# Row scaling in pieces and TensorE transposes ahead of the first projection, with dummy products while x is loaded

## The chip, the cores and the metric

The kernel runs on one core of a Trainium2 chip. The metric is the device time of one execution in microseconds (us); lower is better. The engines are named as the profile names them: PE (TensorE products) and PEld (its weight loads), DVE (VectorE), ACT (ScalarE), POOL (GpSimd), and the queues that issue DMAs (SPq, ACTq, POOLq).

## The reference

One decoder layer on 512 tokens of width 1024, in f32. The part that the change touches is the very beginning:

```
h    = x * rsqrt(mean(x*x, axis=-1) + 1e-6) * attn_norm
proj = h @ w_in     # columns: attention q, k, v | RWKV r, k, v, loras | memory q
```

Behind it come differential attention, an RWKV-7 time mix (a chunked delta-rule recurrence), cross-attention into a normalised memory, one output projection with a residual, and a mixture of 16 experts with top-2 routing. These are the same in both kernels.

## The kernel before, in words

**Arithmetic.** Every large product is computed from pairs: an operand is split into a rounded high part and the rest, and three products (high-high, high-low, low-high) are added in PSUM (`mm3`, L242 to L245; in the first unit written out at L341 to L343). A weight chunk of 128 x 1024 is loaded by SPq into `raw`, ACT copies it into `whi` (L96), DVE subtracts to give `wlo` (L97).

**Beginning.** x is four tiles of 128 tokens by 1024 columns, `xt[0]` to `xt[3]`. Tiles 0 and 1 form half 0, tiles 2 and 3 half 1. For each tile `row_root` (L275) sums the squares (DVE at L279 for one tile of a half, ACT at L281 for the other) and POOL makes the root with a power of -0.5 (L282, L283). PE must turn x so that its columns lie on partitions. The kernel before does this by a product: `half_turn` (L324) multiplies each 128 x 128 block of x with `diag[t]`, a diagonal matrix of the tile's row factors, so that scaling and turning are one f32 product. `diag` is made from the identity by DVE for half 0 (L348) and by ACT for half 1 (L364). One `half_turn(n)` covers 128 columns of the two tiles of a half; n from 0 to 7 is half 0, 8 to 15 is half 1. `half_split` (L330) multiplies the turned block with the norm's gain and splits it into `h_hi` (ACT, L291) and `h_lo` (DVE, L292). `half_products` (L335) then multiplies column block k of a half with the first 256 columns of w_in: six products of 256 columns per k, 48 per half.

**Order.** The block from L345 to L374 stands in a manual schedule: ACT, DVE and PE carry out what is written there in that order. POOL and SPq are not under it. In the kernel before PE's order is: turns 0 to 7, products of half 0 for k 0 to 3, turns 8 to 11, products of half 0 for k 4 to 7, turns 12 to 15, products of half 1. All work behind it (`projections`, `rwkv`, `attention`, the experts) is ordered by a planner that simulates the engines' times, from generators that are woven by estimated delays (`Weave`); the next unit's products (L243 to L245) follow on PE, and a root pair for the memory tile goes through DVE, POOL and ACT (L279, L282, L283, L287). POOL's long list of small preparations (`later()`, L380) may start only when the last root of x is there.

**Banks.** The turned blocks go through six PSUM banks, used by halves: two of `pt`, two of `pc`, two of `pp` (L319). The bank of block n is used again 12 blocks later.

Of the kernel before, what the change touches and what calls it, by code (L numbers as in the profile page):

```python
# [12 lines left out]
BF = mybir.dt.bfloat16  # L13
I32 = mybir.dt.int32
AF = mybir.ActivationFunctionType
ALU = mybir.AluOpType
# [4 lines left out]
P = 128  # L21
S = 512
D = 1024
NT = S // P
KC = D // P
# [125 lines left out]
def hybrid_layer_kernel(ctx, tc, x, mem, positions, cols, w_in, w_kv, w_out, wa2, g2, ffn, wr, br,  # L151
                        wg, wu, wd, out):
    nc = tc.nc
    V, A, G, T = nc.vector, nc.scalar, nc.gpsimd, nc.tensor
# [3 lines left out]
    rc = ctx.enter_context(tc.tile_pool(name="rc", bufs=1))  # L158
# [12 lines left out]
    def pp():  # L171
        return psp.tile([P, 512], F32, name="pp", bufs=4)

    def pc():
        return pools["ps"].tile([P, 512], F32, name="pc", bufs=2)
# [18 lines left out]
    def b4(name, shape, dtype=F32):  # L194
        return biga.tile(shape, dtype, name=name)
# [4 lines left out]
    xt = [xs[t // 2][:, t % 2, :] for t in range(NT)]  # L200
# [4 lines left out]
    ident = const.tile([P, P], F32, name="ident")  # L205
# [69 lines left out]
    def row_root(src, vec=True):  # L275
        ss = wk.tile([P, 1], F32, name="ssx", bufs=4)
        r = wk.tile([P, 1], F32, name="rsx", bufs=4)
        if vec:
            V.tensor_tensor_reduce(b4("aw0", [P, D]), src, src, 1.0, 0.0, op0=ALU.mult, op1=ALU.add, accum_out=ss)  # L279
        else:  # L280
            A.activation(b4("aw1", [P, D]), src, AF.Square, accum_out=ss)  # L281
        G.tensor_scalar(r, ss, 1.0 / D, RMS_EPS, op0=ALU.mult, op1=ALU.add)  # L282
        return r, G.tensor_tensor(r, r, mhalf, op=ALU.pow)  # L283
# [6 lines left out]
    def split_cols(ps, g, hi, lo):  # L290
        first = A.activation(hi, ps, AF.Copy, scale=g)  # L291
        return first, V.scalar_tensor_tensor(lo, ps, g, hi.bitcast(F32), op0=ALU.mult, op1=ALU.subtract)  # L292


    held = [ws.pair.pop() for _ in range(4)]
    ws.pump()
    for t in (2, 3):
        nc.sync.dma_start(xt[t], x[t * P:(t + 1) * P, :])
# [5 lines left out]
    dint = post_[:, S:2 * S]  # L304
    nc.sync.dma_start(posr, bass.AP(tensor=positions.tensor, offset=positions.offset, ap=[[0, P], [1, S]]))
    nc.sync.dma_start(posc, positions.rearrange("o (t p) -> p (o t)", p=P))
    diags = [b4(f"qmT{t}", [P, 2, P]) for t in range(2)]
    diag = [diags[t // 2][:, t % 2, :] for t in range(NT)]
    first_ps = [pp() for _ in range(2)]
    first_w = []  # L310

    def weights():
        ws.pair.append(held.pop())
        ws.pump()
        first_w.append(ws.use())
# [3 lines left out]
    def half_bank(n):  # L319
        if n % 12 < 6 and len(banks) <= n // 12 * 6 + n % 6:  # L320
            banks.append((pt, pt, pc, pc, pp, pp)[n % 6]())
        return banks[n // 12 * 6 + n % 6][:, n % 12 // 6 * 256:n % 12 // 6 * 256 + 256]

    def half_turn(n):  # L324
        hf, k = divmod(n, KC)
        o = half_bank(n)
        for t in range(2):
            T.matmul(o[:, t * P:(t + 1) * P], xt[2 * hf + t][:, k * P:(k + 1) * P], diag[2 * hf + t], start=True, stop=True)

    def half_split(n):  # L330
        hf, k = divmod(n, KC)
        tk = slice(hf * 256, hf * 256 + 256)
        return split_cols(half_bank(n), col[:, C_AN + k:C_AN + k + 1], h_hi[:, k, tk], h_lo[:, k, tk])

    def half_products(hf, ks):  # L335
        tk = slice(hf * 256, hf * 256 + 256)
        for k in ks:
            hi, lo = first_w[k // 4]
            for j in range(2):
                o, wh, wl = first_ps[j][:, tk], hi[:, k % 4, j * P:(j + 1) * P], lo[:, k % 4, j * P:(j + 1) * P]  # L340
                T.matmul(o, wh, h_hi[:, k, tk], start=hf == 0 and k == 0, stop=False, skip_group_check=True)  # L341
                T.matmul(o, wh, h_lo[:, k, tk], start=False, stop=False, skip_group_check=True)
                T.matmul(o, wl, h_hi[:, k, tk], start=False, stop=k == KC - 1, skip_group_check=True)  # L343

    with tc.manual_schedule(engines={mybir.EngineType.Activation, mybir.EngineType.DVE, mybir.EngineType.PE}):  # L345
        roots = [row_root(xt[0]), row_root(xt[1], False)]
        for t in range(2):
            V.tensor_scalar(diag[t], ident, roots[t][0], None, op0=ALU.mult)  # L348
        for n in range(6):
            half_turn(n)  # L350
        weights()
        half_split(0)
        half_split(1)
        for n in (6, 7):
            half_turn(n)
        half_split(2)
        half_split(3)
        weights()
        roots += [row_root(xt[2]), row_root(xt[3], False)]
        half_products(0, range(4))  # L360
        for n in range(4, KC):
            half_split(n)
        for t in (2, 3):
            A.activation(diag[t], ident, AF.Copy, scale=roots[t][0])  # L364
        for n in range(KC, KC + 4):
            half_turn(n)
        half_products(0, range(4, KC))
        half_split(KC)
        half_split(KC + 1)
        for n in range(KC + 4, 2 * KC):  # L370
            half_turn(n)
        for n in range(KC + 2, 2 * KC):
            got_h = half_split(n)
        half_products(1, range(KC))  # L374
# [41 lines left out]
    qmT = [b4(f"qmT{h}", [P, S]) for h in range(2)]  # L416
# [686 lines left out]
    with tc.issue_after(anchor[0].ins):  # L1103
        iota16 = rc.tile([P, 16], F32, name="iota16")
        G.iota(iota16, pattern=[[1, 16]], base=0, channel_multiplier=0, allow_small_or_imprecise_dtypes=True)
        slot1 = rc.tile([P, CAP], F32, name="slot1")
        G.iota(slot1, pattern=[[1, CAP]], base=1, channel_multiplier=0, allow_small_or_imprecise_dtypes=True)
        dum = rc.tile([P, 1], F32, name="dum")
        G.iota(dum, pattern=[[0, 1]], base=S, channel_multiplier=1, allow_small_or_imprecise_dtypes=True)
        tri = rc.tile([P, P], BF, name="tri")  # L1110
        onb = rc.tile([P, P], BF, name="onb")
        G.memset(onb, 1.0)
        G.affine_select(tri, onb, pattern=[[1, P]], compare_op=ALU.is_gt, fill=0.0, base=0, channel_multiplier=-1)
        member = rc.tile([P, NT, NE], BF, name="member")
        rankm = rc.tile([P, NT, NE], F32, name="rankm")
        rhs = rc.tile([P, NT, NE, 6], BF, name="rhs")
        pcol = rc.tile([P, 1], F32, name="pcol")
        G.iota(pcol, pattern=[[0, 1]], base=0, channel_multiplier=1, allow_small_or_imprecise_dtypes=True)
        G.memset(rhs[:, :, :, 2], 1.0)
        G.tensor_copy(rhs[:, :, :, 1], pcol[:, 0:1, None].to_broadcast([P, NT, NE]))  # L1120
        for t in range(NT):
            G.memset(rhs[:, t, :, 0], float(t * P))
# [124 lines left out]
    for z in ORDER.split():  # L1247
        op, t = z[0], int(z[1:] or 0)
# [254 lines left out]
```

## Time and profile before

| what | us |
|---|---|
| median of 3 runs | 627.85 (626.47 to 631.8) |
| the profiled execution | 631.21 |
| its span, first to last instruction | 629.5 |
| PE busy | 603.6 (96%) |
| DVE busy | 496.4 (79%) |
| ACT busy | 413.9 (66%) |
| mean granted TensorE clock | 0.988 |

Busy times are sums over the span. PE's are modelled ends of a pipelined engine, so starts and paces of successive instructions say more than durations: two f32 products that each last 0.28 us can follow one another at 0.12 us. All times below count from the span's first instruction.

### The profile page before, as it was taken

The page shows a single profiled execution, that of the slowest core. Times are in us where ns is not written, and L with a number is a line of the kernel's source. Part 1 is how long each engine was busy: PE and PEld are TensorE (multiplying, and loading weights), DVE is VectorE, ACT ScalarE, POOL GpSimd, SP SyncE. Part 2 cuts the span into 40 slices and gives each one's busy share as a digit, 9 for nine tenths or more (in the row PEclk, how much of TensorE's full clock was granted, in tenths as well). Part 3 has the DMA queues.
Part 4 walks back from the last instruction along what each step waited for, and adds up shares of the span by engine and source line. Part 5 has one row for each costly group of instructions (what it writes and reads, how often), then busy time and mean ns, then how long its engine had stood idle before and what let it go on. Part 6 is the DMA issues. An engine that isn't in the chain of part 4 may idle for free.

```text
span 629.5 us, 11197 instructions
## 1 busy us (share of the span) xinstructions
PE 603.6 (96%) x4130; PEld 486.6 (77%) x4130; DVE 496.4 (79%) x897; ACT 413.9 (66%) x633; POOL 124.0 (20%) x129
## 2 busy tenths in 40 slices
PE   4999999999999999999998999999999999999992
PEld 4968899999988877889996777777777777777771
DVE  5655795699966687555468999999999999988991
ACT  5478433453449675655247788888889888888881
POOL 2710211244400114304002011111011111320001
PEclk9999999999999997999999999999999999999997
DMA  9442333323252030879798999999999999799913
GB/s 303 137 137 67 101 101 98 87 70 99 68 118 69 2 135 1 298 272 348 278 336 278 364 345 371 372 373 355 364 356 361 363 364 373 232 373 375 337 26 54
DMA packets 77502, 144.19 MB, mean 229 GB/s; under 512 B 12832, under 2 KB 30496, under 8 KB 77440
## 3 DMA queue, kind: packets, MB, share of 16 engines
q1 hardware_dynamic: 69344, 126.59, 57.1%
q0 software_dynamic: 3760, 13.24, 8.9%
q10 hardware_dynamic: 4336, 3.57, 1.8%
q8 instruction: 34, 0.56, 0.4%
q14 instruction: 28, 0.23, 0.1%
HBM read 131.72 MB, written 11.67 MB: 228 GB/s over the span
## 4 chain that ended last, share of the span: by engine, by line
PE 82%; DVE 9%; DMA 3%; ACT 2%; issue 2%; POOL 1%; ACTq 0%; POOLq 0%; SPq 0%; DVEq 0%
PE pp L243 14%; PE pp L245 13%; PE pp L244 13%; PE py L244 5%; PE py L245 4%; PE py L243 4%; DVE prod L743 3%; DVE wlo L97 3%; PE pp L1063 3%; PE pp L1064 2%; PE pp L1065 2%; PE pt L986 2%; DVE lor L744 2%; PE pp L1345 1%; PE py L1201 1%
## 5 line engine op out<-in xcount | busy, mean ns | idle before, releaser
L245 PE MATMUL pp<-whi,xl 128*96 128x512 f32 x264 | 104.0, 395 | 0.0
L244 PE MATMUL pp<-wlo,xh 128*96 128x512 f32 x264 | 103.8, 394 | 0.0
L243 PE MATMUL pp<-whi,xh 128*96 128x512 f32 x264 | 101.2, 394 | 0.8 <-ACT xh L1332 0.8
L1393 POOL DMA_INDIRECT out<-ye,sidx x16 | 23.2, 1452 | 226.3 <-DVE gidx L1295 118.7
L96 ACT ACTIVATE whi<-raw 128x1024 fp32r<-128x1024 f32 x42 | 44.1, 1058 | 32.9 <-PE pp L245 24.7
L245 PE MATMUL pp<-whi,hm_l 128*128 128x256 f32 x224 | 63.8, 285 | 0.0
L243 PE MATMUL pp<-whi,hm_h 128*128 128x256 f32 x224 | 63.1, 282 | 0.0
L244 PE MATMUL pp<-wlo,hm_h 128*128 128x256 f32 x224 | 63.1, 282 | 0.0
L97 DVE TENSOR_TENSOR wlo<-raw,whi 128x1024 fp32r<-128x1024 f32 x42 | 53.7, 1284 | 11.2 <-ACT whi L96 10.8
L243 PEld LDWEIGHTS pp<-whi,xh 128*96 128x96 f32 x264 | 42.5, 161 | 19.6 <-ACT xh L1332 1.3
L245 PEld LDWEIGHTS pp<-whi,xl 128*96 128x96 f32 x264 | 42.6, 161 | 18.4
L244 PEld LDWEIGHTS pp<-wlo,xh 128*96 128x96 f32 x264 | 42.5, 161 | 18.2
L244 PE MATMUL py<-wlo,hh 128*96 128x512 f32 x120 | 47.9, 399 | 0.0
L245 PE MATMUL py<-whi,hl 128*96 128x512 f32 x120 | 47.0, 392 | 0.0
L243 PE MATMUL py<-whi,hh 128*96 128x512 f32 x120 | 47.0, 392 | 0.0
L97 DVE TENSOR_TENSOR wlo<-u,whi 128x1024 fp32r<-128x1024 f32 x34 | 40.8, 1224 | 6.2 <-ACT whi L96 6.1
L97 DVE TENSOR_TENSOR wlo<-lraw,whi 128x1024 fp32r<-128x1024 f32 x36 | 42.6, 1219 | 2.7 <-ACT whi L96 2.5
L245 PEld LDWEIGHTS pp<-whi,hm_l 128*128 128x128 f32 x224 | 42.1, 188 | 1.2 <-issue 0.5
L243 PEld LDWEIGHTS pp<-whi,hm_h 128*128 128x128 f32 x224 | 42.0, 188 | 1.0 <-DVE sm L936 0.4
L244 PEld LDWEIGHTS pp<-wlo,hm_h 128*128 128x128 f32 x224 | 42.3, 189 | 0.6 <-issue 0.2
L96 ACT ACTIVATE whi<-lraw 128x1024 fp32r<-128x1024 f32 x36 | 37.1, 1058 | 5.1 <-PE pp L245 3.6
L96 ACT ACTIVATE whi<-u 128x1024 fp32r<-128x1024 f32 x34 | 35.2, 1057 | 6.7 <-PE pp L1065 3.7
(405 smaller groups left out, 1568.5 us busy)
## 6 DMA issues: line engine op xcount, KB each, us to landing
raw<-in_w_in SPq DMA_DIRECT2D x22, 512.0 KB, 3.7
u<-in_wd SPq DMA_DIRECT2D x12, 512.0 KB, 9.4
lraw<-in_wg SPq DMA_DIRECT2D x12, 512.0 KB, 11.2
lraw<-in_wu SPq DMA_DIRECT2D x12, 512.0 KB, 7.5
lraw<-in_wd SPq DMA_DIRECT2D x12, 512.0 KB, 12.4
f<-in_wg SPq DMA_DIRECT2D x11, 512.0 KB, 10.0
u<-in_wu SPq DMA_DIRECT2D x11, 512.0 KB, 12.5
eraw<-in_wd SPq DMA_DIRECT2D x10, 512.0 KB, 13.5
```

The lines of the kernel that those rows point to most:

```text
L96: nc.scalar.activation(hi, slot, AF.Copy)
L97: nc.vector.tensor_sub(lo, slot, hi.bitcast(F32))
L243: T.matmul(ps, ah, bh, start=first, stop=False)
L244: T.matmul(ps, ah, bl, start=False, stop=False)
L245: T.matmul(ps, al, bh, start=False, stop=last)
L743: V.tensor_mul(prod[:, :, 0:n], ud[:, s:s + 1, s:32].to_broadcast([P, 16, n]), zs[:, :, s:32])
L744: V.tensor_reduce(zs[:, :, s], prod[:, :, 0:n], axis=AX.X, op=ALU.add)
L986: T.matmul(po[:, 0:P], aws[i % 2][:, kb * P:(kb + 1) * P], qk["v"][:, kb, h * P:(h + 1) * P], start=kb == 0, stop=kb == qb)
L1063: T.matmul(o, ah, hi[:, k % 4, :], start=k == k0 and i == lead, stop=False, skip_group_check=True)
L1064: T.matmul(o, ah, lo[:, k % 4, :], start=False, stop=False, skip_group_check=True)
L1065: T.matmul(o, al, hi[:, k % 4, :], start=False, stop=k == k1, skip_group_check=True)
L1393: G.indirect_dma_start(out, bass.IndirectOffsetOnAxis(ap=si, axis=0), ye, None, compute_op=ALU.add)
```

## The change

The turn is no longer a product with a diagonal matrix. x is scaled in place, in two pieces of 512 columns per tile: ACT scales the first tile of a half, DVE the second, piece by piece in turn. PE then transposes blocks of the scaled x with the identity. The diagonal matrices are gone. In the manual order, PE has 80 products of 128 x 128 bf16 ones into an otherwise unused bank ahead of everything, while x is loaded; the constant that they read (`onb`, filled by POOL) is made at the beginning instead of late. The roots of tiles 2 and 3 now stand ahead of the second weight chunk, and half 1 is scaled and turned in one go behind the products of half 0.

```
+    onb = rc.tile([P, P], BF, name="onb")
+    G.memset(onb, 1.0)
...
-    diags = [b4(f"qmT{t}", [P, 2, P]) for t in range(2)]
-    diag = [diags[t // 2][:, t % 2, :] for t in range(NT)]
...
-            T.matmul(o[:, t * P:(t + 1) * P], xt[2 * hf + t][:, k * P:(k + 1) * P], diag[2 * hf + t], start=True, stop=True)
+            T.transpose(o[:, t * P:(t + 1) * P], xt[2 * hf + t][:, k * P:(k + 1) * P], ident)
...
+        early = pc()
+        for _ in range(80):
+            T.matmul(early[:, 0:P], onb, onb, start=True, stop=True)
         roots = [row_root(xt[0]), row_root(xt[1], False)]
-        for t in range(2):
-            V.tensor_scalar(diag[t], ident, roots[t][0], None, op0=ALU.mult)
+
+        def half_scale(hf):
+            for i in range(2):
+                cs = slice(i * 512, i * 512 + 512)
+                A.activation(xt[2 * hf][:, cs], xt[2 * hf][:, cs], AF.Copy, scale=roots[2 * hf][0])
+                V.tensor_scalar(xt[2 * hf + 1][:, cs], xt[2 * hf + 1][:, cs], roots[2 * hf + 1][0], None, op0=ALU.mult)
+
+        half_scale(0)
         for n in range(6):
             half_turn(n)
         weights()
...
+        roots += [row_root(xt[2]), row_root(xt[3], False)]
         weights()
-        roots += [row_root(xt[2]), row_root(xt[3], False)]
         half_products(0, range(4))
         for n in range(4, KC):
             half_split(n)
-        for t in (2, 3):
-            A.activation(diag[t], ident, AF.Copy, scale=roots[t][0])
+        half_scale(1)
+        half_products(0, range(4, KC))
         for n in range(KC, KC + 4):
             half_turn(n)
-        half_products(0, range(4, KC))
         half_split(KC)
         half_split(KC + 1)
         for n in range(KC + 4, 2 * KC):
...
-        onb = rc.tile([P, P], BF, name="onb")
-        G.memset(onb, 1.0)
```

## Rows read from the trace of the kernel before

**Rows 1.** The chain that ended last, by engine, share of the span.
```profile
PE 82%; DVE 9%; DMA 3%; ACT 2%; issue 2%; POOL 1%; ACTq 0%; POOLq 0%; SPq 0%; DVEq 0%
```
**Rows 2.** Windows: length, busy (count) of PE, PEld, DVE, ACT, POOL; clock, DMA.
```profile
30.60:60.00 29.40, 29.40 (x125) 21.02 (x124) 15.21 (x21) 24.21 (x38) 3.15 (x6) 1.00 0.39 119
...
118.00:180.00 62.00, 61.38 (x529) 58.99 (x528) 55.24 (x107) 30.94 (x52) 24.29 (x12) 1.00 0.32 91
```
**Rows 3.** Timeline (start, us, engine, line, operation): the constant and the first roots.
```profile
1.66 0.20 POOL L1112 MEMSET onb<- 128x128 bf16 x1
...
7.27 0.58 POOL L283 TENSOR_TENSOR rsx<-rsx,mhalf 128x1 f32<-128x1 f32 x1
...
8.31 0.56 POOL L283 TENSOR_TENSOR rsx<-rsx,mhalf 128x1 f32<-128x1 f32 x1
8.90 0.28 DVE L348 TENSOR_SCALAR qmT<-ident,rsx 128x128 f32<-128x128 f32 x1 [0.40 <-POOL rsx L283]
```
**Rows 4.** Timeline of PE: the first turns.
```profile
8.23 0.80 PE L328 MATMUL pt<-qmT,f 128*128 128x128 f32 x2 [8.23 <-DVE qmT L348]
...
12.39 1.52 PE L328 MATMUL pp<-qmT,f 128*128 128x128 f32 x8
```
**Rows 5.** The chain in order of time (start, us): turns early, roots, turns late.
```profile
10.89 1.72 PE pc L328 x8
...
15.22 1.22 DVE aw L279
...
23.30 0.89 PE pt L328 x8
```
**Rows 6.** Timeline: splits and products of both halves, and the next unit's start.
```profile
15.71 0.85 ACT L291 ACTIVATE hm_h<-pt,col 128x256 fp32r<-128x256 f32 x2
...
17.35 0.28 PE L343 MATMUL pp<-hm_h,wlo 128*128 128x256 f32 x1
...
24.84 0.36 PE L341 MATMUL pp<-hm_h,whi 128*128 128x256 f32 x1
...
25.18 0.93 DVE L292 SCALAR_TENSOR_TENSOR hm_l<-pc,col,hm_h 128x256 fp32r<-128x256 f32 x2
...
30.58 0.40 PE L243 MATMUL pp<-hm_h,whi 128*128 128x512 f32 x1
```
**Rows 7.** Groups by form up to 32 us: busy us, mean ns of one.
```profile
L97 DVE TENSOR_TENSOR wlo<-raw,whi 128x1024 fp32r<-128x1024 f32 x4 | 5.0, 1244 | 0.5 <-ACT whi L96 0.5
...
L96 ACT ACTIVATE whi<-raw 128x1024 fp32r<-128x1024 f32 x4 | 4.1, 1053 | 0.5 <-DMA raw<-in_w_in 0.5
...
L364 ACT ACTIVATE qmT<-ident,rsx 128x128 f32<-128x128 f32 x2 | 0.8, 403 | 1.2 <-POOL rsx L283 1.1
...
L348 DVE TENSOR_SCALAR qmT<-ident,rsx 128x128 f32<-128x128 f32 x2 | 0.6, 286 | 1.4 <-POOL rsx L283 1.4
```
**Rows 8.** Instructions of line 287: duration in ns, least, median, most.
```profile
L287 ACT ACTIVATE kT<-kT,rsx x2: 1153/1154/1154, 32.2 to 36.7; 128x1024 f32<-128x1024 f32 x2
```
**Rows 9.** Groups by form of DVE over the span: a scaling of 512 columns.
```profile
L1390 DVE TENSOR_SCALAR ye<-pp,gslot 96x512 f32<-96x512 f32 x1 | 0.7, 747 | 2.2 <-PE pp L245 2.2
```
**Rows 10.** The chain in order of time: transposes of the memory tile.
```profile
41.95 0.44 PE pt L511 x4
```
**Rows 11.** Timeline of PE: bf16 products of 128 columns on the same constant.
```profile
324.56 0.89 PE L1269 MATMUL pp<-onb 128*128 128x128 bf16 x13
```
**Rows 12.** DMA issues up to 45 us, median us to landing: x tiles.
```profile
f<-in_x SPq DMA_DIRECT2D x3, 512.0 KB, 8.2
```
**Rows 13.** Timeline of POOL: the memory tile's first root.
```profile
31.61 0.56 POOL L283 TENSOR_TENSOR rsx<-rsx,mhalf 128x1 f32<-128x1 f32 x1
```
**Rows 14.** Windows (columns as in rows 2) around the span's one fall of the clock.
```profile
236.00:242.00 6.00, 4.89 (x49) 3.33 (x46) 5.88 (x15) 4.95 (x17) 3.75 (x3) 1.00 0.00 0
242.00:249.00 7.00, 7.00 (x33) 6.06 (x34) 4.80 (x15) 2.28 (x8) 2.86 (x2) 0.51 0.01 2
```
**Rows 15.** Groups by form of DVE from 118 to 180 us: weight splits.
```profile
L97 DVE TENSOR_TENSOR wlo<-raw,whi 128x1024 fp32r<-128x1024 f32 x9 | 13.6, 1507 | 0.0
```

More of the change, by code (lines that the diff above doesn't have):

```diff
@@ L351, in hybrid_layer_kernel @@
         weights()
-        half_split(0)
-        half_split(1)
+        for n in range(2):
+            half_split(n)
         for n in (6, 7):
             half_turn(n)
-        half_split(2)
-        half_split(3)
+        for n in range(2, 4):
+            half_split(n)
+        roots += [row_root(xt[2]), row_root(xt[3], False)]
         weights()
-        roots += [row_root(xt[2]), row_root(xt[3], False)]
         half_products(0, range(4))
```

## The prediction

> **What bounds the kernel now.** I read first the chain that ended last: PE holds 82% of it [rows 1], so time taken from PE early is worth having if PE stays the one that is waited for. Then the windows: from 30.6 to 60 us PE is busy without a gap, while DVE has half of its time free; from 118 to 180 DVE is near full as well [rows 2]. Then the timeline of the first 31 us, where the change lies. PE does nothing until the first root: POOL's power ends at 7.27 + 0.58 = 7.85 for tile 0 and at 8.31 + 0.56 = 8.87 for tile 1 [rows 3], and the first turn starts at 8.23 [rows 4]. From there PE is nearly always at work until the next unit's products begin at 30.58 [rows 6]. That start is my yardstick: what PE gains there is what the change can give.
>
> Two things are slow in it. Every turned block is an f32 product, and in the trace each counts as two records. Eight records take 1.72 us at 10.89 and 0.89 us at 23.30 [rows 5]: 0.215 against 0.111 each, a ratio of 1.94. The clock column shows 1.00 there, but the paces say that TensorE stood at its 1.2 GHz level at first and at 2.4 GHz later; the eight records from 12.39 on take 1.52 [rows 4], so the rise falls into them, some 4.2 to 5.7 us after the first turn.
>
> **Transposes.** A transpose of f32 by the identity is one record: four take 0.44 us [rows 10], 0.11 each. So 32 blocks cost 32 x 0.111 = 3.6 us where 64 records cost 64 x 0.111 = 7.1 us plus what the low clock added (some 19 records ahead of the rise x 0.104 = 2.0).
>
> **Dummies.** 13 bf16 products of 128 columns take 0.89 us [rows 11]; without the last one's tail of about 0.22 that is 0.056 each at 2.4 GHz. At 1.2 GHz no row shows them: the low bound is 0.056 x 1.94 = 0.108, the high bound the f32 record's 0.215 [rows 5]. I take 0.108, the same instruction at the known ratio. The constant is there at 1.86 [rows 3]. If the clock rises 5 us later as it did before, 47 of the 80 run low until 6.9 and 33 high until 8.8; all low, they end at 10.5. Tile 1's first scaled piece is not there before 9.6 (next part), so the dummies cost nothing in the first case, and in the second about what is hidden by the wait for DVE below.
>
> **Scaling.** ACT scales 128 x 128 in 0.403 [rows 7] and 128 x 1024 in 1.154 [rows 8]; between them a piece of 512 is about 0.72. DVE scales 128 x 128 in 0.286 [rows 7] and 96 x 512 out of PSUM in 0.747 [rows 9]; I take 0.7, near the latter because its width is the same. The pieces stand ahead of everything else on ACT and DVE, so all of it counts there:
>
> ACT: pieces of tile 0 from 7.85 to 9.3; first weight copy 1.05 to 10.35; h_hi 0 to 3 at 0.43 each [rows 6] to 12.1; square of tile 3 to 13.15; second copy to 14.2; h_hi 4 to 7 to 15.9; pieces of tile 2 to 17.35.
>
> DVE: pieces of tile 1 from 8.87 to 10.3; first wlo (1.24) behind the copy to 11.6; h_lo 0 to 3 at 0.465 each [rows 6], the first at 12.05, the last at 13.45; squares of tile 2 (1.22 [rows 5]) to 14.7; second wlo to 15.9; h_lo 4 to 7, first 16.4, last 17.8; pieces of tile 3 to 19.2.
>
> Tiles 2 and 3 are issued at about 2.3 and 3.4 and land about 8.2 later [rows 12], by 11.7, before they are asked for. Tile 2's root is done by POOL in under 0.9 after 14.7 (the power's 0.58 and a short step), ahead of ACT's 15.9. SPq's issues do not move; its next weight load waits for the first wlo, 0.8 us later than before, and has many us in hand.
>
> PE: 16 transposes of half 0 end by about 11.3, then a wait for h_lo 0. Products go at (30.58 - 24.84) / 48 = 0.12 [rows 6], 0.72 per k: k 0 to 3 from 12.05 to 14.9. A wait until 16.4 for the second wlo; k 4 to 7 to 19.3 (all of them ended before only around 23). Turns 8 to 15, 16 x 0.111, to 21.1; their splits start at 20 and come every 0.465, so the products of half 1 need not wait: 48 x 0.12 = 5.75, to 26.85.
>
> **The sum.** PE reaches the next unit at 26.85 instead of 30.58: 3.7 us gained. DVE ends its last split at 23.7 instead of 26.05: only 2.4. That second number matters because the memory tile's root (POOL at 31.61 [rows 13], ACT behind it) and the first unit's result go through DVE, POOL and ACT. They set when the RWKV chain starts. So the gain lies between 2.4 and 3.7. I take 3.4, nearer PE's, since PE's queue is full behind this point [rows 2]. Against the profiled 631.21 that is 627.8; that execution lies 3.4 above the median of 627.85, so for the median I say 624.4.
>
> **A rule against it.** The window before the one fall of the clock has PE at work for 4.89 of 6 us in small products and transposes with gaps, at 1.00; then 0.51 for 7 us [rows 14]. So a thinly used PE does lose the clock here. The page "TensorE: Matmul & The Clock Gate" of the Trainium skill, in its part on PE-mode transpose, says that transposes do not count as PE work for the clock in the usual way. By that rule the clock may fall between the last dummy and the first product; the trace neither shows nor excludes it, since its transposes stand among products.
>
> **Rivals.**
>
> *The clock falls again.* From 8.8 to 12.05 PE has under 2 us of transposes and no product. If it falls there, k 0 to 3 cost up to 24 x 0.233 = 5.6 instead of 2.9; with a rise 4.2 to 5.7 us after 12.05 they end near 17.2, k 4 to 7 near 20.1 instead of 19.3. Loss 0.8, with a later rise 1.8, as the wait until 16.4 absorbs the rest. Gain 1.6 to 2.6: about 625.8. For it: rows 14. Against: 33 dummies at full rate stand right before.
>
> *A better order behind.* All later work is ordered by a planner from simulated times, which the change shifts. If the fall of the clock at 242 goes away, half of its 7 us (3.4) is saved on top: 621.0. Anything like it counts here. Nothing in the profile says that it goes.
>
> *A worse order: slower.* From 125 to 179 us DVE carries the steps of a triangular inverse, one behind the other, and nine weight splits of other work stand among them, 1.5 us each [rows 15]. If PE is ahead by 3.7 but this chain is not, more such splits come due inside it. From three more on (4.5 us) the gain is gone: 628.9; five more in all make 631.9. For it: DVE is busy 55 of 62 us there [rows 2]. Against: the work that feeds the chain shifts too.
>
> *The dummies last too long.* At 0.215 each they end at 1.9 + 17.2 = 19.1. From their end the rest takes 1.8 + 2.9 + 2.9 + 1.8 + 0.4 + 5.75 = 15.5, so PE is at 34.6: 4 us slower, 632. The point from which they cost the whole gain is an end at 15, 0.164 each. Against: their weight loads overlap in rows 11.
>
> *The change does not do what it says:* the transposes still take two records. Then half 1's turns cost 1.8 more: 626.2. Rows 10 speak against.
>
> **How the numbers follow.** Forecast 0.50 (623.3 to 626), clock 0.14, better order 0.16, worse order 0.13, dummies 0.04, two records 0.03. A change of 1%, 6.3 us, is about what can be told from none. Faster by that needs 621.6 or less: most of the better orders and a sliver of the forecast, 0.19. Slower needs 634.1: a tail of the worse order, 0.03. The rest, 0.78, is within 1%. The range reaches from 618.5 (a better order with more than the one fall) to 630 (three to four splits more); outside lie about 0.06 below and 0.1 above.
>
> **What would show it.** Right: the first product near 12, L243's first near 26.9, transposes at 0.11, last h_lo near 23.7, dummies ended before 9.6. Wrong: products at over 0.2 us behind 12 (the clock); the first transpose after 11 (dummies); PE at its yardstick early, but the inverse's last step no earlier than before (order); a wait of PE for the lora unit's activations (DVE, POOL and ACT too late).

## The result, and the profile after

The changed kernel takes 623.07 us (622.21 to 623.69, 8 runs), the kernel before 629.43 (626.11 to 633.45, 8 runs) beside it: a ratio of 0.989 [0.9858, 0.9922]. The time lies 1.3 under the forecast of 624.4. The gain, 6.4, is nearly twice the 3.45 that the forecast took off its median of 627.85. By the medians the gain is 1.0%; its interval, 0.8 to 1.4%, is clear of zero. The time is a little under the band from 623.3 to 626 of the main forecast and within the whole range.

The page of the changed kernel, the chain that ended last by engine [rows 1]:

```profile
PE 88%; DVE 3%; DMA 3%; ACT 2%; issue 1%; SPq 0%; POOL 0%; POOLq 0%; ACTq 0%; DVEq 0%
```

PE's share rose from 82 to 88%, and DVE's fell from 9 to 3%. The timeline of the changed kernel's first 30 us [rows 4 to 6], with the bracket giving the idle time before and what ended it:

```profile
1.20 7.01 PE L348 MATMUL pc<-onb 128*128 128x128 bf16 x80 [1.20 <-POOL onb L297]
...
7.85 1.33 ACT L354 ACTIVATE f<-f,rsx 128x512 f32<-128x512 f32 x2 [0.75 <-POOL rsx L283]
...
8.62 0.33 PE L328 MATMUL pt<-ident,f 128*128 128x128 f32 x1 [0.41 <-ACT f L354]
...
8.76 0.88 DVE L355 TENSOR_SCALAR f<-f,rsx 128x512 f32<-128x512 f32 x2 [1.49 <-POOL rsx L283]
...
10.13 0.60 PE L328 MATMUL pp<-ident,f 128*128 128x128 f32 x4
10.16 1.23 DVE L97 TENSOR_TENSOR wlo<-raw,whi 128x1024 fp32r<-128x1024 f32 x1 [0.16 <-ACT whi L96]
...
11.84 0.83 PE L328 MATMUL pt<-ident,f 128*128 128x128 f32 x4 [1.11 <-DVE hm_l L292]
...
12.42 0.37 PE L341 MATMUL pp<-hm_h,whi 128*128 128x256 f32 x1
...
14.01 1.22 DVE L97 TENSOR_TENSOR wlo<-raw,whi 128x1024 fp32r<-128x1024 f32 x1
...
16.73 2.44 DVE L355 TENSOR_SCALAR f<-f,rsx 128x512 f32<-128x512 f32 x2
...
18.50 0.74 PE L328 MATMUL pc<-ident,f 128*128 128x128 f32 x4
...
20.70 0.36 PE L341 MATMUL pp<-hm_h,whi 128*128 128x256 f32 x1
...
21.93 0.87 DVE L292 SCALAR_TENSOR_TENSOR hm_l<-pc,col,hm_h 128x256 fp32r<-128x256 f32 x2
...
26.43 0.40 PE L243 MATMUL pp<-hm_h,whi 128*128 128x512 f32 x1
```

The yardstick, PE's first product of the next unit, is at 26.43 instead of 30.58: 4.15 earlier. The dummies end at 8.2; the second product follows the first at 0.21, the others follow at 0.12. Windows of the changed kernel, the stretches of [rows 2, 14]:

```profile
30.60:60.00 29.40, 29.40 (x138) 22.17 (x137) 16.54 (x22) 26.51 (x40) 4.09 (x5) 1.00 0.31 97
118.00:180.00 62.00, 62.00 (x547) 59.36 (x546) 53.35 (x106) 30.06 (x53) 23.36 (x13) 1.00 0.35 91
...
236.00:242.00 6.00, 6.00 (x60) 4.39 (x56) 4.60 (x11) 4.21 (x16) 4.23 (x2) 1.00 0.83 283
242.00:249.00 7.00, 7.00 (x61) 6.62 (x60) 5.46 (x12) 4.98 (x14) 2.72 (x2) 1.00 1.03 370
```

The clock no longer falls at 242. Groups of the changed kernel by form: DVE's weight splits from 118 to 180 [rows 15], then, from 20 to 70 us, PE's products of the RWKV decay (contraction over 64 partitions):

```profile
L97 DVE TENSOR_TENSOR wlo<-raw,whi 128x1024 fp32r<-128x1024 f32 x9 | 11.3, 1256 | 0.0
...
L617 PE MATMUL pc<-ths,prod 64*128 64x512 f32 x8 | 3.4, 642 | 0.0
```

The same eight in the kernel before are L609 and count 4.5. Its timeline of PE has them in four pairs of records, with other work between one pair and the next (here the first two):

```profile
37.90 1.12 PE L609 MATMUL pc<-ths,prod 64*128 64x512 f32 x2
38.95 0.49 PE L244 MATMUL pp<-hm_l,whi 128*128 128x512 f32 x1
39.37 1.12 PE L609 MATMUL pc<-ths,prod 64*128 64x512 f32 x2
```

In the changed kernel's timeline of PE the first two pairs are one row:

```profile
35.23 1.13 PE L617 MATMUL pc<-ths,prod 64*128 64x512 f32 x4
```

Two products on different halves of the partitions ran side by side, in the time of one: 1.1 us saved. The Trainium skill, "TensorE: Matmul & The Clock Gate", Part 3 on packing small matmuls, says that products in different row groups of the array overlap; these rows agree. They do so only where the planner left nothing between them: in the kernel before a product of the projection stands there (38.95).

**Three parts of the gain.** Between the two profiled executions (631.21 and 623.17) it is 8.0: 4.15 at the start, 3.5 from the fall of the clock (half of 7 us), 1.1 from the pair; 0.7 is given back elsewhere. The middle part is not in every execution. Beside the experiments the kernel before ran 81 times. In 39 executions its mean granted clock was .989 or less, median 631.93; in the other 42 it was above, median 628.22. Of 14 executions of the changed kernel none was under .992. Against the 42 the gain is 5.1, and 4.15 + 1.1 is 5.25. That the two agree proves little: a mean clock of .991 or .992 can still hold a short low stretch (the profiles of bfill and delay below have one near 190 us), and the 16 executions at .994 or more have a median of 627.4, only 4.3 above the changed kernel.

What is inside the 4.15 is known in part. Taking away the dummies costs 0.8 of it (nodum below), taking away the single record 1.3 (prodturn). The other 2.0 belong to the scaling in pieces and to the new order of the start together; no run takes these two apart.

### The profile page after: what moved, and what is told of

It is laid out like the page before. It is cut to its first block, busy times and chain, and to the rows that moved or that the text cites. A ratio compares the mean times of both kernels' runs of the same rounds, so it can differ in the third digit from the quotient of the medians.

```text
span 621.5 us, 11302 instructions
## 1 busy us (share of the span) xinstructions
PE 600.0 (97%) x4178; PEld 483.7 (78%) x4178; DVE 496.9 (80%) x899; ACT 414.8 (67%) x635; POOL 122.9 (20%) x129
## 4 chain that ended last, share of the span: by engine, by line
PE 88%; DVE 3%; DMA 3%; ACT 2%; issue 1%; SPq 0%; POOL 0%; POOLq 0%; ACTq 0%; DVEq 0%
PE pp L243 17%; PE pp L245 17%; PE pp L244 16%; PE py L244 5%; PE py L245 4%; PE py L243 4%; PE pp L1071 2%; PE pp L1072 2%; PE pp L1073 2%; PE pt L994 2%; PE pp L1351 1%; DVE wlo L97 1%; PE py L1207 1%; DMA lraw<-in_wu 1%; PE pl L1174 1%; PE pc L687 1%
## 5 line engine op out<-in xcount | busy, mean ns | idle before, releaser
L243 PE MATMUL pp<-whi,xh 128*96 128x512 f32 x264 | 101.2, 394 | 0.8 <-ACT xh L1338 0.8
L243 PE MATMUL pp<-whi,hm_h 128*128 128x256 f32 x224 | 64.7, 289 | 0.0
L97 DVE TENSOR_TENSOR wlo<-raw,whi 128x1024 fp32r<-128x1024 f32 x42 | 52.2, 1250 | 13.6 <-ACT whi L96 13.1
L243 PEld LDWEIGHTS pp<-whi,xh 128*96 128x96 f32 x264 | 42.5, 161 | 19.6 <-ACT xh L1338 1.3
L243 PE MATMUL py<-whi,hh 128*96 128x512 f32 x120 | 47.0, 392 | 0.0
L243 PEld LDWEIGHTS pp<-whi,hm_h 128*128 128x128 f32 x224 | 42.1, 188 | 2.0 <-issue 1.1
```

The source lines that it names most:

```text
L97: nc.vector.tensor_sub(lo, slot, hi.bitcast(F32))
L243: T.matmul(ps, ah, bh, start=first, stop=False)
```

## The experiments

The planner orders what follows the start from simulated times. Read from the instructions of each kernel, this later order comes in two kinds: one like the kernel before (106 or 107 projection products on PE ahead of the first RWKV norm product), one like the changed kernel (92 there; 83 in prodturn, 91 to 94 in the others). For each kernel the table has its kind, the first L243-product of the next unit and the median; then the executions with a mean clock of .989 or less, the median of the others, and the busy time of the eight decay products. The next unit's start and the decay are read from one profiled execution of each; that of v2 had a low clock at the start.

| kernel | kind | next unit | us, median (runs) | clock low | others | decay |
|---|---|---|---|---|---|---|
| before | before | 30.6 | 629.4 to 630.7 (8 to 30 a series) | 39 of 81 | 628.2 | 4.5 |
| changed | after | 26.4 | 623.07 (8) | 0 | 623.1 | 3.4 |
| changed, second series | after | 26.4 | 623.29 (6) | 0 | 623.3 | 3.4 |
| nodum | after | 27.2 | 624.03 (6) | 0 | 624.0 | 3.4 |
| prodturn | after | 27.8 | 625.01 (7) | 0 | 625.0 | 4.5 |
| dum170 | after | 29.1 | 627.30 (12) | 0 | 627.3 | 4.5 |
| q20 | after | 27.3 | 626.11 (12) | 0 | 626.1 | 4.5 |
| v1 | after | 26.4 | 623.65 (6) | 0 | 623.7 | 3.4 |
| v2 | after | 28.4 | 623.61 (6) | 1 | 623.6 | 3.4 |
| dum40 | after | 26.6 | 623.86 (6) | 4 | 623.4 | 3.4 |
| dumonly | before | 28.9 | 628.23 (12) | 6 | 626.9 | 4.5 |
| q22 | before | 27.5 | 626.83 (12) | 4 | 626.5 | 3.4 |
| delay | before | 30.5 | 631.26 (12) | 7 | 628.5 | 4.5 |
| bfill | before | 30.6 | 629.70 (12) | 1 | 629.5 | 4.5 |

**nodum**, the changed kernel without its dummies:

```
-        for _ in range(80):
-            T.matmul(early[:, 0:P], onb, onb, start=True, stop=True)
```

> The changed kernel without the 80 dummy products; the later order is exactly that of the changed kernel. Theory A (the dummies only take away the low clock of the first turns, and half 0 waits for the splits anyway): 0.5 to 1.5 us slower than the changed kernel, 623.6 to 624.6; the next unit starts near 27.3. Rival (transposes do not bring the clock up, so the first products run long at the low level): 2 to 3 us slower, 625 to 626, the next unit near 29.

Measured 624.03 (623.24 to 625.05), 0.9904 [0.9868, 0.9939]. PE's timeline of nodum:

```profile
8.59 0.47 PE L328 MATMUL pt<-ident,f 128*128 128x128 f32 x1 [8.59 <-ACT f L352]
...
9.97 1.06 PE L328 MATMUL pc<-ident,f 128*128 128x128 f32 x4
...
12.58 0.56 PE L341 MATMUL pp<-hm_h,whi 128*128 128x256 f32 x1
...
14.65 0.41 PE L341 MATMUL pp<-hm_h,whi 128*128 128x256 f32 x1
...
15.19 0.28 PE L341 MATMUL pp<-hm_h,whi 128*128 128x256 f32 x1
```

The ten products up to 14.65 start 0.21 apart, those from 15.06 on 0.12: the clock rose about 6.4 us after the first transpose. The dummies are worth 0.8 at the yardstick and 1.0 in time.

**dumonly**, the kernel before with the dummies alone:

```
+    onb = rc.tile([P, P], BF, name="onb")
+    G.memset(onb, 1.0)
...
+        early = pc()
+        for _ in range(80):
+            T.matmul(early[:, 0:P], onb, onb, start=True, stop=True)
...
-        onb = rc.tile([P, P], BF, name="onb")
-        G.memset(onb, 1.0)
```

> The kernel before with the 80 dummy products alone: turns stay f32 products with the diagonal, later order nearly that of the kernel before. Theory A: the turns of half 0 run at the high clock and end 2 us earlier, but half 1 waits for its roots as before (17.7), so only 0.3 to 1 us arrives at the next unit (29.6 to 30.3) and the time is 628.4 to 629.1. Rival (the clock at the start is most of the gain): 2 us or more, 627.4 or less.

628.23 (625.71 to 633.12), 0.998 [0.9949, 1.0011]. The yardstick gained 1.6, more than expected: each turn there has two records, and most of half 0's were in the low clock before. Half of the runs had a low mean clock; of the others the median is 1.4 under that of before. PE's timeline of dumonly:

```profile
9.91 1.06 PE L330 MATMUL pc<-qmT,f 128*128 128x128 f32 x8
...
12.51 0.36 PE L343 MATMUL pp<-hm_h,whi 128*128 128x256 f32 x1
```

The next eight records start at 10.80, 0.11 each; the first product comes at 12.51, 2.1 earlier than before.

**prodturn**, the changed kernel with the turn as a product:

```
-            T.transpose(o[:, t * P:(t + 1) * P], xt[2 * hf + t][:, k * P:(k + 1) * P], ident)
+            T.matmul(o[:, t * P:(t + 1) * P], xt[2 * hf + t][:, k * P:(k + 1) * P], ident, start=True, stop=True)
```

> The changed kernel, but the scaled blocks are turned by a product with the identity (two records each) instead of a transpose; the later order is nearly that of the changed kernel. Theory A (the single record is what half 1 gains): half 1's turns cost 32 records instead of 16, 1.8 us more, and half 0's another 0.4, so the next unit starts near 28.6 instead of 26.4 and the time is 2.2 us above the changed kernel: 625.3 (624.8 to 625.8). Rival (DVE's splits are the limit and hide the turns): within 0.7 us of the changed kernel, 623.8 or less.

625.01 (624.69 to 625.98), 0.9912 [0.9875, 0.9949]. The yardstick is 1.3 later, so that is what one record instead of two is worth at the start; the time rose by 1.9. The decay products explain the direction of the rest: they no longer stand side by side. PE's timeline of prodturn:

```profile
18.46 1.13 PE L328 MATMUL pc<-ident,f 128*128 128x128 f32 x8
...
36.58 1.12 PE L617 MATMUL pc<-ths,prod 64*128 64x512 f32 x2
37.89 1.12 PE L617 MATMUL pc<-ths,prod 64*128 64x512 f32 x2
```

**delay**, the changed kernel with 74 more dummies behind the products of half 1, so that PE alone is late and ACT's and DVE's start stays early:

```
+        late_ps = pc()
+        for _ in range(74):
+            T.matmul(late_ps[:, 0:P], onb, onb, start=True, stop=True)
```

> The changed kernel with 74 dummy products on PE behind the last product of half 1, 4.1 us: PE starts the next unit near 30.5, as in the kernel before, while ACT and DVE are as early as in the changed kernel. The planner orders the later work as in the kernel before. Theory A (PE's arrival at the next unit carries the gain): the gain is gone, median 628 to 630.5. Rival (DVE and ACT, which are 2.4 us or more ahead, carry it): 626 or less.

631.26 (627.42 to 635.33), 1.0 [0.9965, 1.0035]. The lora activation on DVE was as early as in the changed kernel, 28.3 instead of 34.0, and nothing of the gain was left: without low clocks 628.5 against 628.2 of before. DVE's timeline of delay:

```profile
28.27 1.40 DVE L446 SCALAR_TENSOR_TENSOR lor<-pp,col,lor 128x511 f32<-128x511 f32 x2
```

PE's timeline of delay has the yardstick where the kernel before had it:

```profile
30.47 0.48 PE L243 MATMUL pp<-hm_h,whi 128*128 128x512 f32 x1
```

So PE's arrival carries the gain, and DVE's and ACT's lead alone gives nothing. delay also has the later order of the kernel before, so by itself it doesn't part PE's lateness from that order. dumonly does: it has that order too, and a yardstick 1.6 earlier made it 1.4 faster.

**dum170**, 170 dummies instead of 80 (the loop's count is the only edit):

> The changed kernel with 170 dummy products instead of 80 at the beginning: they end near 13.2 instead of 8.2. The later order is nearly that of the changed kernel. Theory A (from the dummies' end the rest takes some 15.5 to 16.3 us of PE): the next unit starts at 28.7 to 29.5 instead of 26.4, and the time is 2.3 to 3.1 us above the changed kernel, 625.4 to 626.2. Rival (a planned order that differs in a few rows counts for more than the beginning): more than 1 us off that.

627.30 (626.83 to 627.92), 0.9956 [0.993, 0.9983]. PE's timeline of dum170:

```profile
1.20 11.44 PE L348 MATMUL pc<-onb 128*128 128x128 bf16 x170 [1.20 <-POOL onb L297]
12.47 0.60 PE L328 MATMUL pt<-ident,f 128*128 128x128 f32 x4
```

The yardstick is 2.7 later, the time 4.2; of the extra 1.5 the unpaired decay products are 1.1.

**q20 and q22**, the changed kernel with 20 and 22 dummies behind half 1. Their starts are alike, but 20 leave the later order of the changed kind and 22 turn it into the kind of before:

```
+        late_ps = pc()
+        for _ in range(20):
+            T.matmul(late_ps[:, 0:P], onb, onb, start=True, stop=True)
```

> The changed kernel with 20 more dummy products on PE behind the last product of half 1 (about 1.1 us of PE). The planner's order of the later work stays that of the changed kernel but for a few rows. Theory A (about 4 us of the gain come from the beginning, the rest from the later order): 1 us above the changed kernel, 624.2, with the clock at 1.00 around 242. Theory B (all of the gain comes from the beginning and grows on the way): the same, 624.2. It is the partner of the run with 22.

> The same with 22 dummy products: 0.11 us more of PE, but the planner now orders the later work as in the kernel before, but for a few rows. The beginning is the same as with 20. Theory A: 2.5 to 4 us slower than with 20 (626.7 to 628.2), with a fall of the clock near 240 as in the kernel before. Theory B: within 0.5 us of the run with 20.

q20: 626.11 (625.32 to 626.64), 0.9948 [0.9925, 0.9972]. q22: 626.83 (624.74 to 629.4), 0.995 [0.9922, 0.9978]. The medians, 0.7 apart (0.4 without low clocks), lie near theory B. The spreads, 1.3 against 4.7, speak for the other half of theory A: q20 never had a low clock, q22 in 4 of 12. So the low clocks go with the later order; that the order brings more than these isn't shown. Windows of q22:

```profile
236.00:242.00 6.00, 5.14 (x27) 3.87 (x28) 5.42 (x15) 3.30 (x15) 3.40 (x2) 0.72 0.00 0
```

q20 is 3.0 slower than the changed kernel although its yardstick is only 0.8 later. 1.1 of that is the pair of decay products, which stands side by side in q22 and not in q20; 1 us stays open. Between the two profiled executions the difference is 2.2 (625.32 and 623.17), which the yardstick and the pair nearly cover. q22 has the pair, and its yardstick is 1.1 later; without low clocks it is still 3.4 slower than the changed kernel, so there 2.3 stay open.

**bfill**, the kernel before with ten dummies ahead of each of the last four steps of the RWKV recurrence (their constant is made at the beginning, as in dumonly):

```
+            for _ in range(10 if c >= 4 else 0):
+                T.matmul(px[:, 0:P], onb, onb, start=True, stop=True)
```

> The kernel before with 10 dummy products on PE ahead of each of the last four steps of the recurrence (about 225 to 255 us), 40 x 0.056 = 2.2 us of PE if none is hidden; the beginning and the order up to there are those of the kernel before. Theory A (the upper part of the times of the kernel before are executions in which the clock falls near 242): no execution with a mean clock under 0.99, all within 3 us of one another, the median 627.5 to 629.5, under that of the kernel before. Rival (the spread has another cause): the times still reach over 631 and the median is 1 to 2 us above that of the kernel before.

629.70 (628.58 to 635.02), 0.9989 [0.9959, 1.0019]. Windows of bfill:

```profile
188.40:191.80 3.40, 3.40 (x18) 3.40 (x18) 1.49 (x5) 2.61 (x9) 0.00 (x0) 0.50 0.00 0
...
236.00:242.00 6.00, 6.00 (x51) 4.39 (x51) 5.86 (x16) 4.84 (x18) 2.31 (x3) 1.00 0.02 5
242.00:249.00 7.00, 6.46 (x68) 5.19 (x66) 6.88 (x17) 4.20 (x15) 3.46 (x2) 1.00 0.01 2
```

One of 12 executions had a low clock where 39 of 81 had one before. This fits a fall that comes from PE's thin use in these steps and can be bought off. But it isn't the only place: the profile shows a short low stretch at 188, ahead of the filled steps (delay's profile has one from 188.2 to 191.6, q22's one near 204), and the times still spread over 6.4 us where 3 were expected. The dummies cost 1.2 of what they save (629.5 against 628.2), and the median hardly moves.

**again, v1, v2**. The first is the changed kernel once more. In v1 DVE takes the second piece of tile 0 while it waits for the root of tile 1; in v2 turns 6 and 7 moreover stand behind the first products:

```
+            if hf == 0:
+                V.tensor_scalar(xt[0][:, 512:D], xt[0][:, 512:D], roots[0][0], None, op0=ALU.mult)
...
-                A.activation(xt[2 * hf][:, cs], xt[2 * hf][:, cs], AF.Copy, scale=roots[2 * hf][0])
+                if hf == 1 or i == 0:
+                    A.activation(xt[2 * hf][:, cs], xt[2 * hf][:, cs], AF.Copy, scale=roots[2 * hf][0])
...
-        for n in (6, 7):
-            half_turn(n)
...
-        half_products(0, range(4))
+        half_products(0, range(1))
+        for n in (6, 7):
+            half_turn(n)
+        half_products(0, range(1, 4))
```

> The changed kernel once more, beside the two versions below on the same chip. Theory A (the start and the clock near 242 us account for the gain): 622.2 to 623.7 as before, every execution with a mean clock of .992 or more. Rival B (the first series was a lucky one): executions above 626 with a clock under .990 turn up here too.

> In the changed kernel ACT scales both pieces of tile 0 from 7.85 to 9.18 before it copies the first weight, while DVE waits for the root of tile 1 until 8.76. Here DVE takes the second piece of tile 0 (0.44). Theory A (PE's arrival at the next unit is passed on one to one): the copy, the split behind it and the first products come up to 0.6 earlier, DVE's own pieces of tile 1 at most 0.1 later; next unit 25.9 instead of 26.4; 622.6. Rival B (DVE's splits are what PE waits for in half 1, so the start gains nothing): next unit 26.3 to 26.5, 623.1. Rival C (the few rows of the later order that come out differently weigh more than the start): anything from 621 to 625 with the next unit early.

> As v1, and turns 6 and 7, which waited 1.1 us for the split of block 0 in the same bank, are issued behind the first products. Theory A: first product up to 0.8 earlier than in the changed kernel, but the wait for the second weight's split takes most of it back: next unit 25.7 to 25.9, 622.4 to 622.6. Rival B: 26.3 to 26.5 and 623.1, since half 1 waits for DVE. Rival C as for v1.

again: 623.29 (622.69 to 623.44), 0.9888 [0.9858, 0.9918], as in the first series. v1: 623.65 (623.34 to 624.21), 0.9895 [0.9865, 0.9925]: rival B. Timeline of v1, ACT and DVE:

```profile
8.29 1.04 ACT L96 ACTIVATE whi<-raw 128x1024 fp32r<-128x1024 f32 x1
8.87 0.88 DVE L358 TENSOR_SCALAR f<-f,rsx 128x512 f32<-128x512 f32 x2 [0.40 <-POOL rsx L283]
...
10.13 1.23 DVE L97 TENSOR_TENSOR wlo<-raw,whi 128x1024 fp32r<-128x1024 f32 x1
```

ACT's copy starts 0.8 earlier, DVE's split behind it at 10.13 instead of 10.16: DVE's own pieces and small preparations stand ahead of it. DVE sets the pace of the start.

v2: 623.61 (623.07 to 624.67), 0.9893 [0.9863, 0.9924], no gain either. Its profiled execution, 624.67, is the one with a low clock and shows the first rival of the prediction at work. PE's timeline of v2:

```profile
1.20 5.90 PE L348 MATMUL pc<-onb 128*128 128x128 bf16 x80 [1.20 <-POOL onb L297]
8.62 0.33 PE L328 MATMUL pt<-ident,f 128*128 128x128 f32 x1 [1.52 <-ACT f L357]
...
10.85 0.56 PE L341 MATMUL pp<-hm_h,whi 128*128 128x256 f32 x1
12.00 0.58 PE L342 MATMUL pp<-hm_l,whi 128*128 128x256 f32 x1 [0.58 <-DVE hm_l L292]
```

The clock rose early, so the dummies ended at 7.1 instead of 8.2. Windows of v2:

```profile
10.00:11.00 1.00, 1.00 (x11) 1.00 (x9) 0.96 (x4) 1.00 (x3) 0.00 (x0) 0.85 1.04 414
11.00:12.00 1.00, 0.42 (x3) 0.12 (x2) 1.00 (x3) 0.77 (x3) 0.00 (x0) 0.50 1.04 414
```

The clock fell, the products ran 0.21 apart until 17.3, and the yardstick came at 28.4. In the profiles of q20 and delay the dummies ended at 7.1 too, and the clock held: an early end doesn't bring the fall each time, and that it brings it at all rests on this one profiled execution.

**dum40**, 40 dummies instead of 80 (again only the count):

> The changed kernel with 40 dummies instead of 80. At 0.08 each they end near 4.4, and PE is idle until the first transpose at 8.6. In the profile of v2 the 80 dummies ended at 7.1, and the products from 12.4 on ran at 0.214 until 17.3; in the profile of the changed kernel they ended at 8.2 and the products ran at 0.12. Theory A (dummies must reach the transposes; what ends earlier is lost): as without dummies, first product near 12.5, pace 0.21 at first, next unit 27.0 to 28.4, 624 to 624.7. Rival B (once the clock has risen, the thin work up to the products keeps it): next unit 26.4, products at 0.12, 623.1. The later order is row for row that of the changed kernel, so the time follows from the start alone.

623.86 (622.92 to 624.42), 0.9889 [0.9852, 0.9926]. PE's timeline of dum40:

```profile
1.20 4.45 PE L348 MATMUL pc<-onb 128*128 128x128 bf16 x40 [1.20 <-POOL onb L297]
8.52 0.47 PE L328 MATMUL pt<-ident,f 128*128 128x128 f32 x1 [2.88 <-ACT f L354]
...
9.90 1.06 PE L328 MATMUL pc<-ident,f 128*128 128x128 f32 x4
...
13.72 0.29 PE L343 MATMUL pp<-hm_h,wlo 128*128 128x256 f32 x1
```

Between the theories: the transposes ran at the low pace (four records in 1.06, against 0.60), as A says, but the rise came by 13.7, and the yardstick is 0.2 late, not 0.6. The 40 dummies ended at 5.65 and not near 4.4, as they ran at the low pace to the last: 0.107 each, not 0.08. Four of six executions had a mean clock of .988 or .989. Their later order is that of the changed kernel, which never showed one, so the fall presumably lies in the start, where a clock that had risen under the dummies fell in the gap; none of these four was profiled, so this isn't shown.

## Why the prediction was right or wrong

**The start: right, a little short.** The yardstick was forecast at 26.85. The first product came at 12.42 instead of 12.05: turns 6 and 7 write the other halves of the banks of blocks 0 and 1 and waited 1.11 for the split of block 0, which the prediction overlooked. A gap until 16.4 was forecast before k = 4; there was hardly any, since the second weight split ended at 15.2. So half 0's products ended at 18.5 instead of 19.3, and half 1 took the 0.12 a product that was expected. Its turns took 2.2 (18.50 to 20.70) instead of 1.8, and its last split ended at 22.8 instead of 23.7.

**Prices.** A low-clock dummy was taken at 0.108 and a high-clock one at 0.056. In the trace the dummies' starts lie 0.107 apart until 6.2 and 0.056 apart behind it: both prices and the rise after 5 us were right. They began at 1.20 and not at 1.86, since their constant is now made first, so they ended at 8.2 and not at 8.8. ACT's piece was 0.67 (0.72 forecast), DVE's 0.44 (0.7, bounded by 0.286 and 0.747; the row out of PSUM was the wrong neighbour). The second time the same two pieces took DVE 2.44, while POOL filled tiles of zeros (0.95, 0.53 and two of 0.21 from 16.65 to 18.36). The first of the two took 1.91 and ended at 18.63, 0.3 after the last fill; the second, behind the fills, took 0.61. The Trainium skill, "SBUF — State Buffer", section "SBUF: two separate sides", says that DVE and GpSimd lock a shared pair of ports against each other. These rows fit that, and so does dum170, where the first piece began 0.60 behind the first fill instead of 0.08: it took only 1.38 and again ended 0.3 after the last fill. No run took POOL's work away. It cost little: PE was in half 0's products until 18.5, and the first four transposes then took 0.74 instead of 0.60.

**The step that failed: "the gain lies between 2.4 and 3.7".** The lower end took DVE's lead as what the RWKV chain gets. delay showed that this lead alone gives nothing. PE's lead was passed on whole: a later yardstick cost about as much in time, 0.8 and 1.0 in nodum, 1.6 and 1.4 from dumonly to the kernel before. The exceptions are q20 and q22, with 1 and 2.3 us open. The upper end, 3.7, was short as well: the start gave 4.15, and more came on top (next paragraph). The wait that the lower end feared did not arise, because the planner put the lora activation ahead of the memory tile's scaling on ACT. ACT's timeline of the kernel before:

```profile
32.21 1.15 ACT L287 ACTIVATE kT<-kT,rsx 128x1024 f32<-128x1024 f32 x1 [4.72 <-POOL rsx L283]
33.27 1.25 ACT L434 ACTIVATE lor<-pp,ext 128x512 f32<-128x512 f32 x2
```

And of the changed kernel, where DVE's part of it then starts at 28.33 instead of 33.97:

```profile
26.28 1.27 ACT L442 ACTIVATE lor<-pp,ext 128x512 f32<-128x512 f32 x2 [2.30 <-PE pp L343]
...
31.74 1.14 ACT L287 ACTIVATE kT<-kT,rsx 128x1024 f32<-128x1024 f32 x1
```

**The better order: a rival with 0.16, and it came on top.** "Nothing in the profile says that it goes", the prediction says of the fall at 242. It went, in all 14 executions of the changed kernel. Its price was misread too: the 3.4 by which the profiled execution lay above the median is half of 7 us of low clock. The profile was of an execution that had the fall, in a kernel where about half have it. Its absence is worth 3.7 to those and at most a short stretch to the rest. The pair of decay products, 1.1, was not seen at all. Both hang on the later order, which no run changed alone, and neither is what the edit is about.

**The other rivals.** The clock falling again behind the dummies was real but rare: in v2's profile it cost 2.0 at the yardstick and about 1 in time; in none of the 14 executions of the changed kernel does the mean clock show it. The worse order went the other way: from 118 to 180 there are still nine weight splits, at 1.26 instead of 1.5, and the inverse's last copy comes at 163.6 instead of 178.5. Most of that lead is lost again; the end gained 8.0. "Too long" has its size from dum170. Two records are refuted by four transposes between 9.69 and 10.13, 0.11 each.

**The rule that was weighed.** Transposes between the dummies and the products left the clock up in the changed kernel's profile, and it fell in v2's, where the dummies had ended 1.1 earlier. prodturn has products in their place, and there the clock held as well, by its profile and by the mean clock of all 7 executions (.993 or more). So no run shows an effect that is the transposes' own, and none excludes it.

**Why the time came out near 624.4.** Two errors offset each other, so that the hit is luck in part. The gain was too small by 3. The median it was taken from, of three runs of which one (631.8) has the time of a low clock, lay under the 629.4 to 630.7 of the longer series.

## What to carry to other kernels

Where PE holds the chain, a microsecond earlier at its first long queue is a microsecond at the end, and an engine that is merely early beside it gives nothing. Before a profile's time is compared with a median, look whether it holds a fall of the clock that other executions don't have: half of the low stretch may be the whole difference. When a planner orders what follows, look in both traces for what became neighbours by chance (half-height products in pairs, a thin stretch of PE), as such gains can come and go with an edit ahead of them (20 or 22 dummies were enough here).

## What was not expected of the hardware

Under the same 80 dummies the clock rose 2.7 us after PE's start in one profile (v2) and 5.0 in another (the changed kernel); in nodum it took 6.4 from the first transpose. So a fixed number of dummies ends at a different time from execution to execution, from 7.1 (v2) to 8.4 (v1) here. A scaling of 128 x 512 on DVE is 0.44 with POOL quiet; begun just behind POOL's first fill of zeros it took 1.91, until 0.3 after the last. In the profiles of nodum and dum40 the clock column shows 1.00 while records come at the low pace: it shows a fall, not a clock that has yet to rise.
